# The last expert's gate and up weights ahead of expert 30's down weights, and the overflow branch ahead of the last column blocks

## The chip, the core and the metric

The kernel runs on one core of a Trainium2 chip. The metric is the device time of one launch in microseconds (us). A core has engines with instruction streams of their own: PE (TensorE, matrix products; PEld is its weight load, PEq and PEldq its sequencer), DVE (VectorE), ACT (ScalarE), POOL (GpSimd) and SP (SyncE, which here issues the DMAs). An engine executes its stream in order; engines wait for each other on semaphores.

## The reference

One decoder layer on 256 tokens of width 2048: RMSNorm, one input projection, differential attention beside a pooling mixer, one output projection and a residual, a second RMSNorm, a mixture of 32 gated experts, and a final RMSNorm. The part that matters here:

```python
coarse = xt @ w_coarse + b_coarse;  gsel = argmax(coarse)        # one of 4 groups
fine_sel = (xt @ w_fine[g] + b_fine)[tok, gsel]                  # 8 experts of the group
top_v, top_i = lax.top_k(fine_sel, 2)                            # 2 experts per token
for g in range(4):
    hg = einsum('td,edf->tef', xt, w_gate[sl]);  hu = einsum('td,edf->tef', xt, w_up[sl])
    h = silu(hg) * hu * combine[:, sl, None]
    y = y + einsum('tef,efd->td', h, w_down[sl])
return rmsnorm(h + y, final_norm_g)
```

An expert has 4 MB of gate, 4 MB of up and 4 MB of down weights; the 32 experts have 384 MB.

## The kernel before

All weights are streamed in units of 1 MB, 12 for an expert: 8 for gate and up (row tiles j = 0 to 3 of each) and 4 for down. SP issues them in the order of the code into a ring of 17 buffers. DMAs go over 8 semaphore lanes in turn, so the issue of one waits until the one 8 before it has landed.

Each expert has 32 token slots. `gather` brings the tokens of 4 experts together. For an expert `e`:

- `expert_in`: 32 products (tile `gu`) as the gate and up units land; the sums of each go through a copy (`part`) and 4 transposing products (`hT`), then silu and a multiplication give `hs`.
- `way_back`: the small tiles `bk` and `ws` that carry slots back to tokens (tile `pb`).
- `expert_out` (line 687, all experts but the last): 16 products `pd` over the four down units, `weighted` (line 683 on ACT gives `eoh`, line 684 on DVE `eol`), then 16 products `py` (line 699), and 8 additions to `y` on DVE (line 701). `py` uses the 4 PSUM banks of `psB`, so from the fifth on a `py` waits for an addition.

The last expert, 31, is written apart. `GU_ORDER[1]` loads and uses its four gate units before its four up units. Its down weights are cut by columns, not by rows of the sum: three units of 512 columns and two halves of 256. For each block, `down` (line 718) makes `pd31n` and its weighting, and `add_up` (line 727) makes the products and line 728 the additions; `square_sum` (lines 711, 708) sums the squares. `load_root` (line 188) loads the scalar engine's table for the square root ahead, and `keep_warm` puts 40 products that nothing reads on PE. `final_rstd` makes the norm's factor. Then comes the overflow branch: each engine loads the fullest expert's count (line 857) and jumps over `overflow` (line 859) when no expert has more than 32 tokens, which is the case with these inputs. The scaled rows go out at lines 866 and 868.

A scheduler at build time may move instructions within a stretch of code, but not over the branch. On the path that is not taken each engine raises its semaphores by what `overflow` would have added (the EVENT_SEMAPHORE rows of line 859), after its own earlier work is done; what other engines wait for beyond the branch counts from there.

Of the kernel before, what the change touches and what calls it, by code (L numbers as in the profile page):

```python
# [9 lines left out]
F32 = mybir.dt.float32  # L10
# [7 lines left out]
P = 128  # L18
T = 2            # token tiles
S = 256          # tokens  # L20
D = 2048
KT = D // P      # 16
NCK = 512        # columns of a weight chunk
# [3 lines left out]
NG = 4           # expert groups  # L27
EG = 8           # experts of a group
NE = NG * EG
FF = 512  # L30
NR = NG + NE     # router columns
C = 32           # token slots of an expert
EB = P // C      # experts whose slots are gathered at once
EPS = 1e-6
GU_ORDER = ([(j, m) for j in range(4) for m in range(2)], [(j, m) for m in range(2) for j in range(4)])
WINDOWS = (2, 4, 8, 16)
LAM_INIT = 0.8 - 0.6 * math.exp(-0.3 * 0)
N1, N2, N3 = 8, 7, 2     # units of the weight stream: throughout, after in_proj, after out_proj
AHEAD = 3                # steps by which the weights are split before their products
# [3 lines left out]
def hybrid_block(ctx: ExitStack, tc: tile.TileContext, x, xT, par, lam4d, rbias, w_in, pool_w, w_out, w_out_b,  # L43
# [32 lines left out]
    def load_unit(src, name):  # L76
        """Some row tiles of a chunk of weights."""
        u = wunit(name).rearrange("p (k n) -> p k n", k=src.shape[1])
        nc.sync.dma_start(u, src)
        return u  # L80

    # the chunks of columns, in the order of the work: v, q, k, q, k, u, u, and w_out
    views = [w_in[c] for c in (4, 5, 0, 2, 1, 3, 6, 7)] + [w_out[c] for c in range(3)] + [w_out_b[c] for c in range(2)]
    # the order of the row tiles: w_out's wait for the heads and pools
# [37 lines left out]
    def keep_warm(rhs, n, name):  # L122
        """Products that nothing reads: the tensor engine's clock drops when it idles."""
        pw_ = bank(name)
        for _ in range(n):
            nc.tensor.matmul(pw_[:, 0:rhs.shape[-1]], ones_b, rhs, start=True, stop=True)
# [6 lines left out]
    # -dist for (q0,k0) | (q1,k0) (q1,k1)  # L133
# [7 lines left out]
    # tri[s, t] = 1 where s <= t  # L141
# [4 lines left out]
    iota_s = const.tile([P, EB, C], F32, name="iota_s")      # 1 + place, EB times  # L146
    nc.gpsimd.iota(iota_s, pattern=[[0, EB], [1, C]], base=1, channel_multiplier=0,
                   allow_small_or_imprecise_dtypes=True)
    # low[i, j] = 1 where j < i
# [4 lines left out]
    iota_m = const.tile([P, NG], F32, name="iota_m")       # i - 4  # L154
    nc.gpsimd.iota(iota_m, pattern=[[1, NG]], base=-NG, channel_multiplier=0,
                   allow_small_or_imprecise_dtypes=True)
    # sel[32 j + s, s'] = (s == s')
# [5 lines left out]
    def rsqrt(pool, dst, ssq, n, tag):  # L163
        """dst = (ssq / n + eps) ** -0.5, elementwise, by Newton's steps from a bit-level seed."""
        shp = list(ssq.shape)
        a = pool.tile(shp, F32, tag=tag + "a", name=tag + "a")
        nc.vector.tensor_scalar(a, ssq, 1.0 / n, EPS, op0=OP.mult, op1=OP.add)
        h = pool.tile(shp, I32, tag=tag + "h", name=tag + "h")
        nc.vector.tensor_scalar(h, a.bitcast(I32), 1, None, op0=OP.logical_shift_right)
        nc.vector.tensor_scalar(dst.bitcast(I32), h, -1.0, float(0x5F3759DF), op0=OP.mult, op1=OP.add)  # L170
        q = pool.tile(shp, F32, tag=tag + "q", name=tag + "q")
        for _ in range(3):
            nc.vector.tensor_mul(q, dst, dst)
            nc.vector.scalar_tensor_tensor(q, q, -0.5, a, op0=OP.mult, op1=OP.mult)
            nc.vector.scalar_tensor_tensor(dst, q, 1.5, dst, op0=OP.add, op1=OP.mult)

    def rsqrt_of(dst, a, tag):
        """dst = a ** -0.5: the scalar engine's root, the reciprocal, a Newton step."""
        q = const.tile(list(a.shape), F32, tag=tag + "q", name=tag + "q", bufs=2)
        nc.scalar.activation(q, a, AF.Sqrt)  # L180
        nc.vector.reciprocal(dst, q)
        nc.vector.tensor_mul(q, dst, dst)
        nc.vector.scalar_tensor_tensor(q, q, -0.5, a, op0=OP.mult, op1=OP.mult)
        nc.vector.scalar_tensor_tensor(dst, q, 1.5, dst, op0=OP.add, op1=OP.mult)

    def load_root(after):
        """The scalar engine's table for the root, ahead of its use."""
        nc.scalar.activation(const.tile([P, 1], F32, tag="root", name="root", bufs=2), after, AF.Sqrt, scale=0.0)

# [18 lines left out]
    def split(s_):  # L208
        """Weights in two parts that a single pass each carries exactly."""
# [12 lines left out]
    def multiply(s_):  # L222
# [6 lines left out]
        for kk in range(ks):  # L229
# [4 lines left out]
            if c < 2 or c >= 8:            # tokens x columns: the activations stand  # L234
# [5 lines left out]
            else:                          # columns x tokens: the weights stand  # L240
# [7 lines left out]
    # what goes along with each step  # L248
# [8 lines left out]
    # 1 / rms of the tokens, as a column and along the rows  # L257
# [41 lines left out]
    def _():  # L299
        # lambda  # L300
# [7 lines left out]
        # router weights times the norm's gain  # L308
        nc.vector.tensor_tensor(wr, wr, g2c[:, :, None].to_broadcast([P, KT, NR]), op=OP.mult)
        # 1 / (t + 1) of the first tokens  # L310
# [7 lines left out]
    def evac_qk(c, i):  # L318
        """Half i (0 queries, 1 keys) of the heads 4 c to 4 c + 3."""
# [9 lines left out]
    def scores(h):  # L329
# [14 lines left out]
        nm = front.tile([P, 2, 2], F32, tag="nm", name=f"nm{h}", bufs=2)       # [t, c]  # L344
# [202 lines left out]
    # the group: the first of the largest  # L547
# [13 lines left out]
    # an expert's rank: how many are larger, or as large and earlier  # L561
# [18 lines left out]
    slot = small("slot", T, NE)         # 1 + place among the expert's tokens, or 0  # L580
    nc.vector.tensor_tensor(slot, pos[:, 0:2 * NE].rearrange("p (t e) -> p t e", t=T), mskf, op=OP.mult)

# [4 lines left out]
    # where the stream's units go: what is free early first; the y tiles follow the units in mpool  # L587
# [12 lines left out]
    def load_expert(e):  # L600
        gu, ds = ([], []), []
        for j, m in GU_ORDER[e == NE - 1]:
            for v in ((gate_v, up_v)[m],):
                gu[m].append(unit(f"w{'gu'[m]}{e}_{j}").rearrange("p (k f) -> p k f", k=4))
                nc.sync.dma_start(gu[m][-1], v[e, :, 4 * j:4 * j + 4, :])
        for j in range(4):
# [3 lines left out]
            else:  # L610
                ds[-1] = ds[-1].rearrange("p (f n) -> p f n", f=4)
                for c0 in range(0, NCK, NCK if j < 3 else NCK // 2):
                    cs = slice(c0, c0 + (NCK if j < 3 else NCK // 2))
                    nc.sync.dma_start(ds[-1][:, :, cs],
                                      down_v[e, :, :, j * NCK + cs.start:j * NCK + cs.stop].rearrange("f p n -> p f n"))
        return gu, ds

    def gather(b):
        """The slots of EB experts: their tokens' rows, transposed; in four steps."""
# [18 lines left out]
    def expert_in(e, xe, gu, step=None):  # L638
        """silu(x gate) * (x up), transposed."""
        i = e % EB  # L640
        acc = [psA.tile([P, 512], F32, tag="acc", name=f"gu{e}{m}") for m in range(2)]
        for j, m in GU_ORDER[e == NE - 1]:
# [17 lines left out]
    def way_back(e):  # L660
        """[slot, token] EB times, and the slots' weights."""
# [14 lines left out]
    def weighted(pd, ws_, n, name, last=False):  # L676
        """The slots' outputs times their weights, in two parts that a single pass each carries exactly."""
# [35 lines left out]
    def down(e, hs, ds, ws_, n):  # L713
        """Some columns of the last expert's way out, in four parts of the sum over f."""
# [7 lines left out]
    def add_up(e, bk, eo, n, t):  # L722
        """The way back adds the parts up."""
# [12 lines left out]
    def overflow(hnT):  # L736
        """Tokens beyond an expert's slots: every expert over all tokens, weighted by what the slots left out."""
# [9 lines left out]
        for t in range(T):  # L747
# [34 lines left out]
            for n in range(5):  # L782
                square_sum(t, n)
        final_rstd()

    ws = {0: load_expert(0)}
    xe, step, routed = gather(0)
    keep_warm(hot, 18, "warm2")
    ws[1] = load_expert(1)
    y = [mpool.tile([P, D], F32, tag="m", name=f"y{t}", bufs=4) for t in range(T)]  # L790
    hs0 = expert_in(0, xe, ws[0][0], step)

    def weigh():
        """Weights of the chosen experts, and the fullest expert's count."""
# [29 lines left out]
    for e in range(NE):  # L824
        if 1 < e + 1 < NE:
            ws[e + 1] = ws.get(e + 1) or load_expert(e + 1)
# [4 lines left out]
        gu, ds = ws.pop(e)  # L831
        hs = expert_in(e, xe, gu) if e else hs0
        bk, ws_ = way_back(e) if e else bk0
        if e < NE - 1:
            expert_out(e, hs, ds, bk, ws_)
        if e == NE - 4:
            # the last norm's gain, on all partitions
            gf = mpool.tile([P, D], F32, tag="m", name="gf", bufs=4)
            for n in range(4):
# [5 lines left out]
                nc.scalar.copy(gf[:, n * NCK:(n + 1) * NCK], pgf)  # L845
    load_root(hs[:, 0, 0:1])
    ss3 = const.tile([P, T], F32, name="ss3")
    rstd3 = const.tile([P, T], F32, name="rstd3")
    keep_warm(ones_b, 40, "warm3")
# [7 lines left out]
    n_most = nc.values_load(most_i[0:1, 0:1], min_val=0, max_val=S)  # L857
    hnT = mpool.tile([P, KT, P], F32, tag="m", name="hnT", bufs=4)
    with tc.If(n_most > C):
        overflow(hnT)  # L860

# [13 lines left out]
def _layout(i):  # L875
    """The inputs as the kernel reads them: rows and columns moved, nothing computed."""
    import numpy as np
    a = {k: np.asarray(v) for k, v in i.items()}
    rows = lambda v: v.reshape(P, KT)                  # d = p * 16 + k
    tiles = lambda v: v.reshape(-1, P).T               # d = k * 128 + p  # L880
# [41 lines left out]
```

## Time and profile before

| | us |
|---|---|
| three timed runs, median | 1266.39 (1266.08 to 1267.1) |
| span of the profiled execution | 1267.7 |
| last SP weight issue (last half unit of expert 31's down weights) | 1235.5 |
| first `pd31` product | 1242.57 |
| last sum of squares on ACT ends | 1255.27 |
| first scaled row on DVE | 1257.71 |

The page gives no total for the profiled execution beside its span, which is 1.3 us above the median of the timed runs. PE is busy 87% of the span and the 16 DMA engines carry 365 GB/s on average, but the average hides three stages: the projections (PE and DVE), the experts (the weight stream), and the tail after the last weights. Times of rows below count from the start of the span.

### The profile page before, as it was taken

To read this page: it belongs to the slowest core of one execution; us is meant where nothing else is said; L and a number is where in the kernel's file an instruction comes from. 1 tells how busy PE (TensorE), PEld (TensorE's weight loads), DVE (VectorE), ACT (ScalarE), POOL (GpSimd) and SP (SyncE) were. 2 spreads that over 40 slices of the span, in tenths; PEclk is the share of its full clock that TensorE was granted. 3 is DMA by queue.
4 is the path that set the end of the run, shared out by engine and by line. 5 is a ranking of instruction groups with operands and counts; after the bars stand their busy time and mean duration, and the time that the engine had idled before them with its cause. 6 is when DMAs were issued, how large, how long until landed. Compare 5 with 4: busy or idle time off the path is not lost. (4 is left out here: it accounts for less than half of the span.)

```text
span 1267.7 us, 17150 instructions
## 1 busy us (share of the span) xinstructions
PE 1102.7 (87%) x7043; PEld 651.6 (51%) x7043; DVE 498.9 (39%) x1046; ACT 232.7 (18%) x503; POOL 2.1 (0%) x13
## 2 busy tenths in 40 slices
PE   9999999999998988887788779877977888888875
PEld 6899999889733622442263326323632352244222
DVE  6657788654342223232232222222332313222325
ACT  6545555444000000000000000000000000000103
POOL 0000000000000000000000000000000000000000
PEclk9999999999998979898779877977997787879977
DMA  9954443795899999999999999999999999999994
GB/s 375 357 179 167 159 142 134 298 370 207 335 420 421 420 421 421 421 421 421 421 420 421 421 422 422 420 421 421 421 421 421 421 420 421 421 421 421 421 412 146
DMA packets 67957, 464.10 MB, mean 366 GB/s; under 512 B 7584, under 2 KB 8992, under 8 KB 12576
## 3 DMA queue, kind: packets, MB, share of 16 engines
q1 hardware_dynamic: 67728, 462.92, 89.9%
q8 instruction: 57, 0.93, 0.3%
q14 instruction: 28, 0.23, 0.0%
q10 hardware_dynamic: 144, 0.01, 0.0%
HBM read 460.81 MB, written 2.10 MB: 365 GB/s over the span
## 5 line engine op out<-in xcount | busy, mean ns | idle before, releaser
L647 PE MATMUL gu<-wg,xe 128*32 128x512 f32 x1024 | 211.7, 651 | 14.8 <-DMA wg<-in_w_gate_dram 14.8
L647 PE MATMUL gu<-wu,xe 128*32 128x512 f32 x1024 | 196.7, 650 | 9.9 <-DMA wu<-in_w_up_dram 9.9
L691 PE MATMUL pd<-wd,hs 128*32 128x512 f32 x992 | 157.5, 787 | 25.9 <-DVE hs L657 19.3
L219 DVE TENSOR_TENSOR wlo<-w,whi 128x512 fp32r<-128x512 f32 x192 | 131.1, 689 | 82.3 <-ACT whi L218 81.5
L701 DVE TENSOR_TENSOR y<-y,py 128x512 f32<-128x512 f32 x240 | 148.2, 681 | 31.1 <-PE py L699 30.2
L218 ACT CAST whi<-w 128x512 fp32r<-128x512 f32 x192 | 117.9, 619 | 116.7 <-PE acc L246 56.7
L654 PEld LDWEIGHTS hT<-sel,part 128*128 128x128 f32 x512 | 74.6, 224 | 112.8 <-DVE part L652 56.5
L654 PE MATMUL hT<-sel,part 128*128 128x32 f32 x512 | 82.1, 309 | 45.6 <-DVE part L652 23.6
L632 PEld LDWEIGHTS pg<-ohr,h 128*128 128x128 f32 x512 | 112.7, 311 | 6.4 <-DVE y L701 3.9
L632 PE MATMUL pg<-ohr,h 128*128 128x128 f32 x512 | 114.7, 393 | 0.0
L671 DVE CAST bk<-pb 128x256 fp32r<-128x256 f32 x32 | 13.6, 425 | 256.7 <-PE pb L669 256.7
L699 PE MATMUL py<-eoh,bk 32*128 32x512 f32 x248 | 78.0, 550 | 41.1 <-ACT eoh L683 25.0
L652 ACT COPY part<-gu 128x512 f32<-128x512 f32 x32 | 18.8, 586 | 500.3 <-PE gu L647 500.3
L246 PE MATMUL acc<-xhi,whi 128*128 128x256 f32 x384 | 110.1, 287 | 0.0
L246 PE MATMUL acc<-xhi,wlo 128*128 128x256 f32 x384 | 108.7, 283 | 0.0
L246 PE MATMUL acc<-xlo,whi 128*128 128x256 f32 x384 | 108.4, 282 | 0.0
L684 DVE SCALAR_TENSOR_TENSOR eol<-pd,ws,eoh 128x512 fp32r<-128x512 f32 x31 | 23.3, 750 | 192.8 <-ACT eoh L683 192.8
L691 PEld LDWEIGHTS pd<-wd,hs 128*32 128x32 f32 x992 | 35.9, 138 | 122.8 <-issue 79.6
L647 PEld LDWEIGHTS gu<-wg,xe 128*32 128x32 f32 x1024 | 42.1, 114 | 102.9 <-issue 64.6
L699 PEld LDWEIGHTS py<-eoh,bk 32*128 32x128 f32 x248 | 30.7, 199 | 114.7 <-DVE y L701 59.4
L647 PEld LDWEIGHTS gu<-wu,xe 128*32 128x32 f32 x1024 | 40.0, 115 | 77.8 <-issue 54.1
L246 PEld LDWEIGHTS acc<-xhi,whi 128*128 128x128 f32 x384 | 72.6, 189 | 2.4 <-ACT aT L366 2.0
(213 smaller groups left out, 1114.7 us busy)
## 6 DMA issues: line engine op xcount, KB each, us to landing
wg<-in_w_gate_dram SPq DMA_DIRECT2D x128, 1024.0 KB, 19.8
wu<-in_w_up_dram SPq DMA_DIRECT2D x128, 1024.0 KB, 19.8
wd<-in_w_down_dram SPq DMA_DIRECT2D x127, 1024.0 KB, 19.8
w<-in_w_in_dram SPq DMA_DIRECT2D x31, 1024.0 KB, 5.7
w<-in_w_out_dram SPq DMA_DIRECT2D x12, 1024.0 KB, 4.9
w<-in_w_out_b_dram SPq DMA_DIRECT2D x4, 1024.0 KB, 6.0
x<-in_x_dram SPq DMA_DIRECT2D x2, 1024.0 KB, 18.4
h<-in_x_dram SPq DMA_DIRECT2D x2, 1024.0 KB, 8.5
```

The lines of the kernel that those rows point to most:

```text
L218: nc.scalar.copy(hi, w)
L219: nc.vector.tensor_sub(lo, w, hi.bitcast(F32))
L246: nc.tensor.matmul(o, l, r, start=b, stop=e, skip_group_check=True)
L632: nc.tensor.matmul(pg_[:, kk * P:(kk + 1) * P], ht[t][:, 4 * k4 + kk::KT], ohr[:, t].rearrange("p e s -> p (e s)"), start=(t == 0), stop=( ...
L647: nc.tensor.matmul(acc[m][C * kk:C * (kk + 1), :], xe[:, 4 * j + kk, i * C:(i + 1) * C], gu[m][j][:, kk, :], start=(j == 0), stop=(j == 3))
L652: (nc.scalar.copy if m == 0 else nc.vector.tensor_copy)(part, acc[m])
L654: nc.tensor.matmul(hT[:, m, f, :], part[:, f * P:(f + 1) * P], sel, start=True, stop=True)
L671: nc.vector.tensor_copy(bk, pb[:, 0:S].rearrange("p (t s) -> p t s", t=T))
L684: nc.vector.scalar_tensor_tensor(lo, pd[:, 0:n], ws_, hi.bitcast(F32), op0=OP.mult, op1=OP.subtract)
L691: nc.tensor.matmul(pd[C * n:C * (n + 1), :], hs[:, f, :], ds[f][:, n * NCK:(n + 1) * NCK], start=(f == 0), stop=(f == 3))
L699: nc.tensor.matmul(ps, bk[rows, t, :], eo[i][rows, :], start=(i == 0), stop=(i == 1))
L701: nc.vector.tensor_add(y[t][:, cs], (ht if e == 0 else y)[t][:, cs], ps)
```

## The change

The loads of an expert are cut into `load_in` (gate, up) and `load_out` (down). For expert 31, `load_in` stands right behind `load_in(30)`, ahead of `load_out(30)`; its gate and up units alternate like every other expert's. In the loop, `expert_in(31)` and `way_back(31)` stand ahead of `expert_out(30)`. The branch stands behind `expert_out(30)` and ahead of the last expert's column blocks. The 40 products of `keep_warm` are gone. The sums of squares and `final_rstd` inside `overflow` are gone, since the ordinary ones now follow it. Comments are removed.

```diff
-GU_ORDER = ([(j, m) for j in range(4) for m in range(2)], [(j, m) for m in range(2) for j in range(4)])
+GU_ORDER = [(j, m) for j in range(4) for m in range(2)]
...
-            for n in range(5):
-                square_sum(t, n)
-        final_rstd()
...
-    for e in range(NE):
-        if 1 < e + 1 < NE:
-            ws[e + 1] = ws.get(e + 1) or load_expert(e + 1)
+    for e in range(NE - 1):
+        if 1 < e + 1 < NE - 1:
+            ins[e + 1] = load_in(e + 1)
+            if e + 1 == NE - 2:
+                ins[NE - 1] = load_in(NE - 1)
+            outs[e + 1] = load_out(e + 1)
+        if e == NE - 2:
+            outs[NE - 1] = load_out(NE - 1)
...
-        if e < NE - 1:
-            expert_out(e, hs, ds, bk, ws_)
+        if e == NE - 2:
+            hs_z = expert_in(NE - 1, xe, ins.pop(NE - 1))
+            bk_z, ws_z = way_back(NE - 1)
+        expert_out(e, hs, outs.pop(e), bk, ws_)
...
+    n_most = nc.values_load(most_i[0:1, 0:1], min_val=0, max_val=S)
+    hnT = mpool.tile([P, KT, P], F32, tag="m", name="hnT", bufs=4)
+    with tc.If(n_most > C):
+        overflow(hnT)
+    e, hs, bk, ws_, ds = NE - 1, hs_z, bk_z, ws_z, outs.pop(NE - 1)
     load_root(hs[:, 0, 0:1])
-    keep_warm(ones_b, 40, "warm3")
     eo = down(e, hs, ds, ws_, 0)
     for n in range(5):
         nxt = down(e, hs, ds, ws_, n + 1) if n < 4 else None
         for t in range(T):
             add_up(e, bk, eo, n, t)
         eo = nxt
     final_rstd()
-    n_most = nc.values_load(most_i[0:1, 0:1], min_val=0, max_val=S)
-    hnT = mpool.tile([P, KT, P], F32, tag="m", name="hnT", bufs=4)
-    with tc.If(n_most > C):
-        overflow(hnT)
```

PE before, behind expert 30's last up unit (`wu30_3`); `pd30` and `py30` are expert 30's way out:

```order
L647 MATMUL gu301_8338<-wu30_3_8187,xe7_7984 32x512 x4
L654 MATMUL hT30_8371<-sel_165,part1_30_8378 128x32 x4
L691 MATMUL pd30_8399<-wd30_0_8189,hs30_8384 32x512 x4
L691 MATMUL pd30_8399<-wd30_1_8191,hs30_8384 32x512 x4
L691 MATMUL pd30_8399<-wd30_2_8193,hs30_8384 32x512 x4
L691 MATMUL pd30_8399<-wd30_3_8195,hs30_8384 32x512 x4
L699 MATMUL py30_00_8420<-eoh30_8416,bk30_8395 128x512
```

PE at the same place now:

```order
L651 MATMUL gu301_8338<-wu30_3_8187,xe7_7984 32x512 x4
L658 MATMUL hT30_8371<-sel_165,part1_30_8378 128x32 x4
L651 MATMUL gu310_8399<-wg31_0_8189,xe7_7984 32x512 x4
...
L651 MATMUL gu311_8400<-wu31_3_8203,xe7_7984 32x512 x4
L658 MATMUL hT31_8433<-sel_165,part1_31_8440 128x32 x4
L695 MATMUL pd30_8461<-wd30_0_8205,hs30_8384 32x512 x4
L695 MATMUL pd30_8461<-wd30_1_8207,hs30_8384 32x512 x4
L695 MATMUL pd30_8461<-wd30_2_8209,hs30_8384 32x512 x4
L695 MATMUL pd30_8461<-wd30_3_8211,hs30_8384 32x512 x4
```

All of expert 31's gate and up work has moved ahead of expert 30's way out. PE before, at the first column block (`pd310`, `pd311`):

```order
L647 MATMUL gu311_8453<-wu31_3_8326,xe7_7984 32x512 x4
L654 MATMUL hT31_8486<-sel_165,part1_31_8493 128x32 x4
L718 MATMUL pd310_8559<-wd31_0_8328,hs31_8499 32x512 x4
L718 MATMUL pd311_8567<-wd31_1_8330,hs31_8499 32x512 x4
L727 MATMUL py31_00_8575<-eo31_0_8564,bk31_8510 128x512 x2
```

PE now, from expert 30's last products over the branch to the same block (what is left out is `overflow`):

```order
L703 MATMUL py30_13_8510<-eoh30_8478,bk30_8395 128x512
L703 MATMUL py30_13_8510<-eol30_8479,bk30_8395 128x512
L854 TENSOR_LOAD most_i_3857
L856 COMPARE_AND_BRANCH
...
L856 UNCONDITIONAL_BRANCH
L722 MATMUL pd310_9134<-wd31_0_8328,hs31_8446 32x512 x4
L722 MATMUL pd311_9142<-wd31_1_8330,hs31_8446 32x512 x4
L731 MATMUL py31_00_9150<-eo31_0_9139,bk31_8457 128x512 x2
```

What stands right ahead of the first block was the gate and up work of the same expert; now it is the way out of expert 30 and the jump. ACT before, at the last sum of squares and the root of the final norm:

```order
L711 ACTIVATE sq331_8645,ssq3_3872<-y1_3744 128x256
L711 ACTIVATE sq340_8651,ssq3_3872<-y0_3743 128x256
L180 ACTIVATE n3q_8661<-ss3_8516 128x2
L857 TENSOR_LOAD most_i_3857
L859 COMPARE_AND_BRANCH
```

ACT now, behind the branch and at the same place:

```order
L856 UNCONDITIONAL_BRANCH
L687 ACT_TABLE_LOAD
L687 ACTIVATE eo31_0_9139<-pd310_9134,ws31_8459 128x512
...
L715 ACTIVATE sq340_9226,ssq3_3872<-y0_3743 128x256
L180 ACT_TABLE_LOAD
L180 ACTIVATE n3q_9236<-ss3_9132 128x2
L925 UNCONDITIONAL_BRANCH
```

`load_root`'s table load stays ahead of the branch; two more table loads stand behind it, one before the first block and one before the root.

## Rows read from the trace of the kernel before

**Rows 1.** The page: bandwidth in 40 equal slices of the span.

```profile
GB/s 375 357 179 167 159 142 134 298 370 207 335 420 421 420 421 421 421 421 421 421 420 421 421 422 422 420 421 421 421 421 421 421 420 421 421 421 421 421 412 146
```

**Rows 2.** Stretches: length, busy time by engine, granted clock, DMA share, GB/s.

```profile
core 0: us, PE busy (x) PEld busy (x) DVE busy (x) ACT busy (x) POOL busy (x), PEclk, DMA share, GB/s
1190.00:1200.00 10.00, 8.32 (x62) 2.59 (x61) 5.00 (x8) 0.69 (x1) 0.00 (x0) 1.00 1.02 422
1215.00:1220.00 5.00, 2.39 (x11) 0.49 (x11) 0.47 (x1) 0.69 (x1) 0.00 (x0) 0.61 1.01 416
1220.00:1225.00 5.00, 4.65 (x15) 1.28 (x12) 3.36 (x6) 0.00 (x0) 0.00 (x0) 0.50 1.01 419
1246.00:1247.00 1.00, 1.00 (x4) 0.65 (x2) 0.34 (x1) 0.20 (x1) 0.00 (x0) 0.60 0.04 15
```

**Rows 3.** Timeline, SP: the issue of expert 31's last up unit; line 605: its landing.

```profile
1216.78 0.33 SPq L605 DMA_DIRECT2D wu<-in_w_up_dram  x1
...
DMA to landing us min/median/max: 19.7/19.7/19.7
```

**Rows 4.** Timeline, expert 31's last up products to its first column block and norm.

```profile
1237.20 2.78 PE L647 MATMUL gu<-wu,xe 128*32 128x512 f32 x24
1242.21 1.28 ACT L188 ACT_TABLE_LOAD   x1
1242.57 2.90 PE L718 MATMUL pd<-wd,hs 128*32 128x512 f32 x16 [0.69 <-DVE hs L657]
1243.51 0.20 ACT L188 ACTIVATE root<-hs 128x1 f32<-128x1 f32 x1
1252.24 1.80 PE L727 MATMUL py<-eo,bk 128*128 128x256 f32 x8
1255.08 0.19 ACT L711 ACTIVATION_READ_ACCUMULATOR sq<-y 128x1 f32 x1
1255.84 0.20 ACT L180 ACTIVATE n3q<-ss 128x2 f32<-128x2 f32 x1 [0.57 <-DVE ss L733]
1257.71 5.39 DVE L866 SCALAR_TENSOR_TENSOR y<-y,rstd,gf 128x256 f32<-128x256 f32 x8 [0.89 <-DVEq L859]
```

**Rows 5.** Timeline, the way out of expert 30.

```profile
1216.76 1.94 PE L691 MATMUL pd<-wd,hs 128*32 128x512 f32 x8 [2.26 <-DMA wd<-in_w_down_dram]
1218.81 0.69 ACT L683 ACTIVATE eoh<-pd,ws 128x512 fp32r<-128x512 f32 x1 [8.11 <-PE pd L691]
1221.16 3.08 DVE L701 TENSOR_TENSOR y<-y,py 128x512 f32<-128x512 f32 x5 [0.88 <-PE py L699]
1223.05 1.92 PE L647 MATMUL gu<-wg,xe 128*32 128x512 f32 x2
1226.16 1.88 DVE L701 TENSOR_TENSOR y<-y,py 128x512 f32<-128x512 f32 x3 [1.92 <-PE py L699]
```

**Rows 6.** Timeline, the way out of expert 29.

```profile
1189.86 3.64 PE L691 MATMUL pd<-wd,hs 128*32 128x512 f32 x32 [0.69 <-DVE hs L657]
1195.68 5.03 DVE L701 TENSOR_TENSOR y<-y,py 128x512 f32<-128x512 f32 x8 [0.59 <-PE py L699]
1198.39 0.55 PE L699 MATMUL py<-eol,bk 32*128 32x512 f32 x3
```

**Rows 7.** Lines 857 and 859, the branch: engine, instruction, duration in ns, start.

```profile
L857 PEldq TENSOR_LOAD <-most_i x1: 487/487/487, 1253.4 to 1253.4; - x1
...
L859 SPq COMPARE_BRANCH  x1: 50/50/50, 1237.4 to 1237.4; - x1
L859 PEldq COMPARE_BRANCH  x1: 3862/3862/3862, 1254.0 to 1254.0; - x1
L859 ACTq COMPARE_BRANCH  x1: 45/45/45, 1256.4 to 1256.4; - x1
L859 DVEq COMPARE_BRANCH  x1: 72/72/72, 1257.3 to 1257.3; - x1
L859 PEldq EVENT_SEMAPHORE  x1: 51/51/51, 1257.9 to 1257.9; - x1
```

More of the change, by code (lines that the diff above doesn't have):

```diff
@@ L598, in unit, with load_in, load_out @@
         return pool.tile([P, 2048], F32, tag=r, name=name, bufs=bufs)
[L600 to L605, printed above, removed]
+    def load_in(e):
+        gu = ([], [])
+        for j, m in GU_ORDER:
+            gu[m].append(unit(f"w{'gu'[m]}{e}_{j}").rearrange("p (k f) -> p k f", k=4))
+            nc.sync.dma_start(gu[m][-1], (gate_v, up_v)[m][e, :, 4 * j:4 * j + 4, :])
+        return gu
+    def load_out(e):
+        ds = []
         for j in range(4):
@@ L609, in load_expert @@
                 nc.sync.dma_start(ds[-1], down_v[e, j])
[L610 to L616, printed above, removed]
+                continue
+            ds[-1] = ds[-1].rearrange("p (f n) -> p f n", f=4)
+            w = NCK if j < 3 else NCK // 2
+            for c0 in range(0, NCK, w):
+                nc.sync.dma_start(ds[-1][:, :, c0:c0 + w],
+                                  down_v[e, :, :, j * NCK + c0:j * NCK + c0 + w].rearrange("f p n -> p f n"))
+        return ds
     def gather(b):
@@ L641, in expert_in @@
         acc = [psA.tile([P, 512], F32, tag="acc", name=f"gu{e}{m}") for m in range(2)]
-        for j, m in GU_ORDER[e == NE - 1]:
+        for j, m in GU_ORDER:
             if step and m == 0:
@@ L781, in overflow @@
                     nc.vector.scalar_tensor_tensor(y[t][:, cs], po, ccol, y[t][:, cs], op0=OP.mult, op1=OP.add)
-            for n in range(5):
-                square_sum(t, n)
-        final_rstd()
-    ws = {0: load_expert(0)}
+    ins, outs = {0: load_in(0)}, {0: load_out(0)}
     xe, step, routed = gather(0)
     keep_warm(hot, 18, "warm2")
-    ws[1] = load_expert(1)
+    ins[1], outs[1] = load_in(1), load_out(1)
     y = [mpool.tile([P, D], F32, tag="m", name=f"y{t}", bufs=4) for t in range(T)]
-    hs0 = expert_in(0, xe, ws[0][0], step)
+    hs0 = expert_in(0, xe, ins.pop(0), step)
     def weigh():
@@ L830, in hybrid_block @@
                 step(j)
-        gu, ds = ws.pop(e)
-        hs = expert_in(e, xe, gu) if e else hs0
+        hs = expert_in(e, xe, ins.pop(e)) if e else hs0
         bk, ws_ = way_back(e) if e else bk0
-        if e < NE - 1:
-            expert_out(e, hs, ds, bk, ws_)
+        if e == NE - 2:
+            hs_z = expert_in(NE - 1, xe, ins.pop(NE - 1))
+            bk_z, ws_z = way_back(NE - 1)
+        expert_out(e, hs, outs.pop(e), bk, ws_)
         if e == NE - 4:
```

## The prediction, made before the changed kernel was run

> **What bounds the kernel now.** I read the page's 40 slices first. From the twelfth slice on the bandwidth stands at 420 to 422 GB/s until the last two slices [rows 1]: the experts are bound by the weight stream. A unit of 1.049 MB takes 1.049 / 421 = 2.49 us there. The change moves no byte in or out, so what it can win or lose lies behind the point where the stream ends. The stretches by engine come next: between 1246 and 1247 us the stream is at 15 GB/s, so it is over [rows 2], and the span ends at 1267.7. These 21 us are the tail, and only they can move.
>
> In the tail I read the timeline backwards from the first scaled row at 1257.71 [rows 4]. It follows the branch on DVE (0.89 us of idle time), the norm's root on ACT at 1255.84, the last sum of squares, which ends at 1255.08 + 0.19 = 1255.27, and the column blocks, which begin at 1242.57. Before that first product stands the chain of expert 31: its up products end at 1237.20 + 2.78 = 1239.98, then copy, transposes, silu. The last up unit had landed at 1216.78 + 19.7 = 1236.48 [rows 3]. So from the last gate or up unit to the first column block there are 1242.57 - 1236.48 = 6.1 us, then 12.7 us of blocks, then the norm, the branch and the output.
>
> **The change part by part.** *Order of the stream.* Expert 31's eight units come ahead of expert 30's four. All 12 have the same size and the same contiguous lines, and the buffers that they and the last down units reuse were last read by expert 30's gate and up products or earlier work. I cost the swap itself at nothing: expert 30's last down unit takes the place of expert 31's last up unit and lands at 1236.48; expert 31's down units keep their places and the stream its end. Expert 31's last up unit now lands four units earlier, about 1226.5, and its `hs` is ready some 4 us later (about 1 us of products, then the 2.6 us that lay between 1239.98 and 1242.57), well ahead of need.
>
> *The 6.1 us chain goes.* Behind the landing at 1236.48 there is no gate or up work left.
>
> *What is late next.* PE works in order, and expert 30's way out now stands there. Its price has two rows. In the way out of expert 30 before, the last down unit's products began at 1216.76 and the first addition at 1221.16, 4.40 us later; five additions took 3.08 us, 0.62 each [rows 5]. That was at a granted clock of 0.50 to 0.61, its lower level (1.2 GHz) for most of the stretch, behind a PE that had waited for weights: 2.39 us busy in the 5 us from 1215 [rows 2]. In the way out of expert 29, at a granted clock of 1.00, the last quarter of the `pd` products began at about 1189.86 + 0.75 x 3.64 = 1192.6 and the additions at 1195.68, 3.1 us later; all eight took 5.03 us, and PE was through at 1198.39 + 0.55 = 1198.94, 1.77 us before the last of them [rows 2, 6]. After the change PE waits for one unit every 2.49 us from about 1236.5 - 11 x 2.49 = 1209 on, with four products for each, as it did before the stretch at the lower level; without the 40 filler products (they filled time in which PE waited, and cost nothing) it is idle even more. So I take the lower level: first addition at 1236.48 + 4.40 = 1240.9, last one done at 1240.9 + 8 x 0.62 = 1245.8, PE through at 1245.8 - 1.77 = 1244.0. In rows 5 the last three additions came late because PE had products of expert 31 in between (1223.05); these are gone. At the upper level it would be 1239.6, 1244.6 and 1242.8.
>
> *The branch on PE.* This is a wait that the change puts on the path. Before, PE reached the branch when it had nothing more to do: its last product ended at 1252.24 + 1.80 = 1254.04, the jump lasted 3862 ns, and PE was behind it at 1257.95, 3.9 us after its last product [rows 7]. ACT, DVE and SP jumped in 45 to 72 ns. PE is the one with several hundred instructions to jump over. Now all column blocks are queued behind this jump, and ACT and DVE wait for them. I carry the 3.9 us over: first block at 1244.0 + 3.9 = 1247.9. The bounds: 0.1 us if PE jumps like the others; then DVE decides, which must finish its additions and its own branch (0.89 us) first, at 1245.8 + 0.9 = 1246.7. On the other side, a second stop of the same length, if the code behind the jump does not come in one piece or comes slower beside the stream: 1251.8. I take the one row that shows PE at this jump.
>
> The Trainium skill ("Advanced Engine Details and Errata", Control Flow Timing) has a compare-and-branch at about 108 ns. The trace is below that on three engines and 36 times above it on PE; by the page the first block would begin where DVE lets it, and the sum below would be 1.2 us smaller.
>
> *The other engines at the branch.* ACT is through early, since its last work ahead of it is the weighting of expert 30. SP has only the output behind it. DVE's 0.9 us end by 1246.7, under PE's jump. Cost: nothing, while PE's jump lasts; without it DVE's is the one that shows, as said.
>
> *The blocks.* The same instructions as before, by data that has landed before 1247 [rows 2], 12.7 us. Two things can differ. The first 16 products took 2.90 us; at the lower level they take twice 1.94 = 3.9 [rows 5], at the upper one half of 3.64 = 1.8 [rows 6]. PE comes out of 4 us without a product, so I expect the lower level at the start and add 0.5 us, with -1.1 and +2 as the bounds (the last one if the lower level lasts through more blocks; the end of the blocks is paced by the sums of squares on ACT, which don't hang on it).
>
> *The end.* The branch is gone from DVE's path between the norm's factor and the first scaled row: -0.89 + 0.03 = -0.86. But ACT now loads a table between its last sum of squares and the root: `load_root`'s load is followed by a second one behind the branch, which stands early and is hidden, and a third at the root. Last sum 1255.27 + 1.28 = 1256.55, where the root ran at 1255.84 before: +0.71. Together -0.15.
>
> The Trainium skill ("ScalarE: Activation LUTs", What ACT_TABLE_LOAD costs) gives a switch 2.66 us, the load of 1.28 and a drain of 1.38. The trace has the 1.28, and the next activation at 1243.51 begins 0.02 us behind it [rows 4], so no drain shows here; with it the sum would be 1.4 us larger.
>
> **The sum.** First block 1247.9 instead of 1242.57: +5.3. Blocks +0.5, end -0.15: +5.7. The profiled span would be 1273.4 instead of 1267.7. The median of the timed runs, 1266.39, is 1.3 us below that span, and the page shows no other total; the same 5.7 us on the median give **1272.1 us**, slower by 0.45%.
>
> **The rivals.**
>
> *The jump is cheap on PE.* For it: the three other engines in the rows jump in under 0.1 us [rows 7], and the row of 3862 ns is from an engine with nothing left to do. Against: PE alone skips so much code. First block 1246.7, +4.1 + 0.5 - 0.15: 1270.8.
>
> *PE keeps the upper clock.* For it: the way out of expert 29 ran at 1.00. Against: PE was busy 8.32 of the 10 us around it, and only 2.39 of 5 in the paced stretch at 1215, which is the nearer likeness [rows 2]. PE through at 1242.8, first block 1246.7, +4.1, blocks -0.8: 1269.5.
>
> *PE stops twice for code* or longer, beside the end of the stream. +3.9 on the forecast: 1276.0. The trace of before has one such stop only, at a time without traffic.
>
> *Not slower: the chain that goes is what counts.* One mechanism: `hs` of expert 31 is there by 1231, so the blocks run as their units land, and expert 30's way out with the jump fits into the 6.1 us that the old chain took. Place: PE between 1236.5 and the first block. If the first block stays at 1242.6, the blocks run at the upper level (-0.8) and the end wins 0.15: 1265.4. It decides if PE is past the jump by about 1243.5; up to 1245.9 the result stays within 0.2%. Against it: the best row of a way out, at the full clock, needs 6.3 us on PE from the last landing (3.1 + 5.03 - 1.77), and its jump comes on top.
>
> **How the numbers follow.** Forecast 0.50, cheap jump 0.13, upper clock 0.14, two stops 0.15, not slower 0.08. Within 0.2% (2.5 us, about what a measurement of this kernel can tell from no change) means 1263.9 to 1268.9. "Not slower" gives 0.03 to faster and 0.05 to the same, and 0.03 of the upper clock falls below 1268.9. So faster 0.03, same 0.08, slower 0.89. The range from 1268.6 to 1276.6 leaves out most of the last rival below and a part of the two stops above.
>
> **What would show it.** In the new trace: the last down unit of expert 30 lands near 1236.5, and its way out on DVE ends near 1246; PE's COMPARE_BRANCH lasts near 3.9 us and ends near 1248; the first block follows it at once; a table load of 1.28 us stands between ACT's last sum of squares and the root; the first scaled row follows the factor without a branch. The stream's rate and end don't move. I am wrong if PE's jump is short, if the way out ends by 1243, or if the stream ends more than 1 us elsewhere.

## The result and the profile after

The changed kernel took 1274.28 us (median; 1272.71 to 1275.71), the kernel before beside it 1266.24 (1265.8 to 1267.1). The ratio is 1.0064 [1.0049, 1.0078]: slower by 8.0 us, with 6.2 to 9.9 as the interval. The forecast was 1272.1, the range 1268.6 to 1276.6. In the experiments below, one slow execution of e7 (1944 us) is left out of its ratio.

The traced execution has a span of 1273.5 us and was timed at 1275.71, so 2.2 us lie outside the span. Three of its stretches, to be held against [rows 2]:

```profile
1215.00:1220.00 5.00, 4.36 (x36) 0.87 (x28) 0.00 (x0) 0.00 (x0) 0.00 (x0) 0.84 1.02 419
...
1231.00:1236.00 5.00, 4.49 (x24) 2.45 (x28) 0.75 (x2) 1.76 (x3) 0.00 (x0) 0.50 0.98 365
...
1244.00:1248.00 4.00, 0.36 (x1) 0.00 (x0) 1.81 (x4) 0.00 (x0) 0.00 (x0) 0.50 0.13 40
```

From 1231 to 1236, where expert 30's 32 `pd` products begin, the granted clock is 0.50, the lower level; from 1237 to 1243, the rest of that way out, it is 1.00. Between 1244 and 1248 PE works 0.36 us: a hole that the kernel before had only behind its last product. The timeline of the same stretch, which answers to [rows 4, 5]; the first row is SP's, the issue of expert 31's five down units:

```profile
1218.29 17.38 SPq L618 DMA_DIRECT2D wd<-in_w_down_dram  x5
...
1228.77 1.93 PE L651 MATMUL gu<-wu,xe 128*32 128x512 f32 x8
...
1231.52 1.91 PE L658 MATMUL hT<-sel,part 128*128 128x32 f32 x8 [0.81 <-DVE part L656]
...
1233.36 5.45 PE L695 MATMUL pd<-wd,hs 128*32 128x512 f32 x32
...
1238.89 0.69 ACT L687 ACTIVATE eoh<-pd,ws 128x512 fp32r<-128x512 f32 x1 [3.63 <-PE pd L695]
...
1239.98 1.28 ACT L687 ACT_TABLE_LOAD   x1 [0.41 <-DMA wd<-in_w_down_dram]
...
1240.94 4.87 DVE L705 TENSOR_TENSOR y<-y,py 128x512 f32<-128x512 f32 x8 [0.59 <-PE py L703]
...
1243.81 0.55 PE L703 MATMUL py<-eol,bk 32*128 32x512 f32 x1
...
1248.18 3.64 PE L722 MATMUL pd<-wd,hs 128*32 128x512 f32 x16 [3.81 <-PEq L856]
...
1261.37 0.19 ACT L715 ACTIVATION_READ_ACCUMULATOR sq<-y 128x1 f32 x1
1261.58 1.28 ACT L180 ACT_TABLE_LOAD   x1
1262.87 0.20 ACT L180 ACTIVATE n3q<-ss 128x2 f32<-128x2 f32 x1
...
1263.89 5.39 DVE L874 SCALAR_TENSOR_TENSOR y<-y,rstd,gf 128x256 f32<-128x256 f32 x8
```

Read it at the brackets: the first column block at 1248.18 waited 3.81 us for PE's own sequencer at line 856, the branch. The branch itself, by line (engine, duration in ns, start), which answers to [rows 7]:

```profile
L856 ACTq COMPARE_BRANCH  x1: 45/45/45, 1239.4 to 1239.4; - x1
...
L856 PEldq COMPARE_BRANCH  x1: 3794/3794/3794, 1244.1 to 1244.1; - x1
L856 DVEq COMPARE_BRANCH  x1: 72/72/72, 1245.0 to 1245.0; - x1
```

The Trainium skill ("Runtime: NRT & Kernel Launch", Instruction fetch mechanics) says that a taken branch to code that is not yet in the engine's instruction memory stalls until it is fetched, and gives no price. The trace agrees; the price on PE here is 3.35 to 3.86 us in nine of the eleven traces that jump over all of `overflow`, and 6.23 and 6.28 us in the other two (e6, e2).

### The profile page after: what moved, and what is told of

It is laid out like the page before. It is cut to its first block, busy times and chain, and to the rows that moved or that the text cites. A ratio compares the mean times of both kernels' runs of the same rounds, so it can differ in the third digit from the quotient of the medians.

```text
span 1273.5 us, 17081 instructions
## 1 busy us (share of the span) xinstructions
PE 1108.1 (87%) x7003; PEld 650.6 (51%) x7003; DVE 498.5 (39%) x1046; ACT 235.2 (18%) x505; POOL 2.1 (0%) x13
## 5 line engine op out<-in xcount | busy, mean ns | idle before, releaser
L651 PE MATMUL gu<-wg,xe 128*32 128x512 f32 x1024 | 223.3, 665 | 13.4 <-DMA wg<-in_w_gate_dram 13.4
L651 PE MATMUL gu<-wu,xe 128*32 128x512 f32 x1024 | 206.4, 659 | 8.8 <-DMA wu<-in_w_up_dram 8.8
L705 DVE TENSOR_TENSOR y<-y,py 128x512 f32<-128x512 f32 x240 | 148.1, 681 | 37.8 <-PE py L703 37.4
L658 PE MATMUL hT<-sel,part 128*128 128x32 f32 x512 | 80.6, 306 | 45.6 <-DVE part L656 23.6
L703 PE MATMUL py<-eoh,bk 32*128 32x512 f32 x248 | 81.2, 575 | 41.4 <-ACT eoh L687 24.1
```

Of the source, the lines that this page charges most:

```text
L651: nc.tensor.matmul(acc[m][C * kk:C * (kk + 1), :], xe[:, 4 * j + kk, i * C:(i + 1) * C], gu[m][j][:, kk, :], start=(j == 0), stop=(j == 3))
L658: nc.tensor.matmul(hT[:, m, f, :], part[:, f * P:(f + 1) * P], sel, start=True, stop=True)
L703: nc.tensor.matmul(ps, bk[rows, t, :], eo[i][rows, :], start=(i == 0), stop=(i == 1))
L705: nc.vector.tensor_add(y[t][:, cs], (ht if e == 0 else y)[t][:, cs], ps)
```

## The experiments

Executions start their stream up to 2 us apart, so traces are compared from one event: the issue of expert 31's first down unit (the SP row above). The table gives, in us behind that issue, the first column block, the first scaled row and the end of the span; each is one subtraction in a trace.

| kernel | issue | block | scaled | end | ratio to before, timed |
|---|---|---|---|---|---|
| before, trace of the prediction | 1219.09 | 23.5 | 38.6 | 48.6 | |
| before, second (e8) | 1217.71 | 21.1 | 36.3 | 46.2 | 1.0006 [0.9994, 1.0017] |
| before, third (e9) | 1218.37 | 21.1 | 37.0 | 47.1 | 0.9999 [0.9988, 1.0010] |
| changed | 1218.29 | 29.9 | 45.6 | 55.2 | 1.0064 [1.0049, 1.0078] |
| changed, second (e10) | 1218.10 | 29.7 | 44.2 | 53.9 | 1.0059 [1.0036, 1.0082] |
| order alone (e1) | 1216.94 | 24.6 | 40.8 | 50.8 | 1.0022 [1.0003, 1.0040] |
| branch alone (e2) | 1218.95 | 30.7 | 44.8 | 54.5 | 1.0057 [1.0036, 1.0079] |
| branch alone, no filler (e6) | 1217.59 | 27.2 | 42.1 | 51.8 | 1.0035 [1.0022, 1.0048] |
| changed, root behind branch (e3) | 1218.86 | 30.3 | 43.9 | 53.5 | 1.0048 [1.0033, 1.0063] |
| changed, short jump (e4) | 1218.81 | 28.0 | 43.4 | 52.6 | 1.0030 [1.0013, 1.0047] |
| before, no filler (e5) | 1217.99 | 21.9 | 37.4 | 47.2 | 1.0004 [0.9995, 1.0013] |
| changed, filler back (e7) | 1216.98 | 28.5 | 44.3 | 53.9 | 1.0048 [1.0035, 1.0062] |

**e1: the new order, the branch at the end as before.**

```diff
+            for n in range(5):              # back inside overflow
+                square_sum(t, n)
+        final_rstd()
...
-    n_most = nc.values_load(...)        # ahead of the column blocks
...
-    with tc.If(n_most > C):
-        overflow(hnT)
...
     final_rstd()
+    n_most = nc.values_load(...)
...
+    with tc.If(n_most > C):
+        overflow(hnT)
```

> The changed kernel with the branch put back to the end (the sums of squares inside the overflow put back too): only the order of loads and work is new, and the filler products are gone. Theory (way out of expert 30 and PE's jump each carry a part): the first column block starts when PE is through with expert 30's products, near 1244.4 us by the trace, 1.8 us later than before; no table load at the root, and the branch is back on DVE in front of the first scaled row (0.9 us). Time +2 to +3 us against the kernel before, ratio 1.0015 to 1.0025. Rival A (the order alone is what costs, PE's jump is hidden beside it): +5 us or more, ratio above 1.004. Rival B (the order is a gain, only the jump costs): below 0.999.

Measured 1270.21 us, by the ratio +2.8 [0.4, 5.1]: as the theory had it, though the interval just reaches Rival A's +5. Its timeline:

```profile
1234.38 1.07 PE L695 MATMUL pd<-wd,hs 128*32 128x512 f32 x8 [1.44 <-DMA wd<-in_w_down_dram]
...
1237.87 4.87 DVE L705 TENSOR_TENSOR y<-y,py 128x512 f32<-128x512 f32 x8 [0.88 <-PE py L703]
...
1241.55 3.64 PE L722 MATMUL pd<-wd,hs 128*32 128x512 f32 x16
```

Here expert 30's last products wait for the landing and take 1.07 us; PE goes from the way out straight into the block. Without the jump the new order costs 3.5 us at the first block (24.6 against 21.1). One thing besides the branch differs from the changed kernel's trace: the granted clock while PE does expert 31's gate and up work. The same stretch here, then in the changed kernel:

```profile
1224.00:1234.00 10.00, 6.59 (x54) 2.91 (x53) 1.47 (x4) 1.76 (x3) 0.00 (x0) 1.00 1.02 401
```

```profile
1224.00:1234.00 10.00, 8.45 (x42) 5.13 (x38) 1.41 (x4) 1.10 (x3) 0.00 (x0) 0.50 1.01 402
```

It is 0.50 to 0.51 in all five traces with the new order and the new place of the branch (changed, e10, e3, e4, e7). PE is through with expert 30's products 24.7 us behind the issue here, and 26.1 and 26.2 us in the two traces of the changed kernel.

**e2: the old order, the branch ahead of the blocks.**

```diff
-            for n in range(5):              # inside overflow
-                square_sum(t, n)
-        final_rstd()
...
+    n_most = nc.values_load(...)
...
+    with tc.If(n_most > C):
+        overflow(hnT)
     load_root(hs[:, 0, 0:1])
...
     keep_warm(ones_b, 40, "warm3")
...
     final_rstd()
-    n_most = nc.values_load(...)
...
-    with tc.If(n_most > C):
-        overflow(hnT)
```

> The kernel before with nothing changed but the branch, which stands ahead of the last expert's column blocks. Theory: PE jumps for 3.8 us right behind the last up products' transposes (about 1241.9), so the first block starts near 1245.8 instead of 1242.6, +3.2; the blocks start at the lower clock, +0.5; a table load in front of the root and no branch there, -0.15. Time +3 to +4.5 us, ratio 1.0024 to 1.0036. Rival A (the order carries all): within 0.5 us, ratio about 1.000. Rival B (the branch carries all): +5.5 us or more, ratio above 1.0043.

Measured 1274.25, +7.2 [4.6, 10.0]: more than expected, and the price that Rival B named. The timeline shows the two reasons that the expectation missed:

```profile
1236.38 1.07 PE L647 MATMUL gu<-wu,xe 128*32 128x512 f32 x8 [1.48 <-DMA wu<-in_w_up_dram]
...
1245.31 4.42 PE L126 MATMUL warm<-ones_b 128*128 128x128 bf16 x40 [5.98 <-PEq L845]
1249.67 2.70 PE L718 MATMUL pd<-wd,hs 128*32 128x512 f32 x16
```

The jump took 6.28 us, and the 40 products that nothing reads now stood behind it: 4.4 us at the lower clock, on the path.

**e6: e2 without those 40 products.**

```diff
-    keep_warm(ones_b, 40, "warm3")
```

> Order of the kernel before, the branch ahead of the column blocks, and the 40 products that nothing reads left out. With them this kernel had a jump of 6277 ns (1238.9 to 1245.2), the filler behind it for 4.4 us and the first block at 1249.67. Theory (the jump and the filler add up on PE): first block near 1245.2 to 1245.5, limited by the end of the jump, 4.2 us earlier; end of the run 3 to 4 us earlier than with the filler, ratio to the kernel before 1.002 to 1.0035. Rival (the filler only fills a wait for something else, for example DVE's and SP's own way past the branch): first block near 1248 or later, ratio 1.0045 to 1.006.

Measured 1271.39, +4.4 [2.8, 6.1]; the upper end of the theory's range. PE's branch in e6, by line:

```profile
L845 PEldq COMPARE_BRANCH  x1: 6234/6234/6234, 1238.2 to 1238.2; - x1
```

The first block came right behind it, at 1244.75, behind the issue 0.6 to 0.9 us later than expected. So the branch alone costs 6.1 us at the block (27.2 against 21.1), the jump being the long one.

**e4: most of the products in `overflow` left out, so that the jump is short.** This leaves out part of the computation on the path that these inputs don't take.

```diff
-        for t in range(T):
+        for t in range(1):
-            for k4 in range(4):
+            for k4 in (0, 3):
-                    for k in range(KT):
+                    for k in (0, KT - 1):
-                    for f in range(4):
+                    for f in (0, 3):
```

> The changed kernel with most of the overflow's products left out (one token tile, 2 of 16 row tiles, half of the way out), so that the code that PE jumps over is about a tenth; the branch isn't taken with these inputs. Theory (the 3.8 us are the fetch of code far away): PE's COMPARE_BRANCH falls below 0.2 us, the first block then waits for DVE's additions and branch and starts near 1246.3 instead of 1248.2; time about -2 us against the changed kernel, ratio near 1.003 to 1.0045. Rival (PE's jump costs the same whatever its length, since PE first has to drain): COMPARE_BRANCH near 3.8 us, no change.

Measured 1271.38, 2.9 us below the changed kernel's median in the first comparison and 2.1 below that in the last; the ratio, 1.0030, lies within what the theory gave. By line:

```profile
L856 PEldq COMPARE_BRANCH  x1: 368/368/368, 1245.0 to 1245.0; - x1
...
L856 DVEq COMPARE_BRANCH  x1: 72/72/72, 1245.8 to 1245.8; - x1
L856 DVEq EVENT_SEMAPHORE  x1: 21/21/21, 1246.8 to 1246.8; - x1
```

and the first block in its timeline:

```profile
1246.84 3.64 PE L722 MATMUL pd<-wd,hs 128*32 128x512 f32 x16 [1.72 <-DVEq L856]
```

The branch instruction is the same and PE's work ahead of it too; only the code skipped is shorter (32 products instead of 320), and 3794 ns became 368, not quite the 200 that the theory had as its upper end. Now PE stands 1.72 us for DVE's own way past the branch, so only half of the 3.4 us comes back (first block at 28.0 against 29.9). In the 5 us from 1244 the instruction queue q8 moved two packets in the changed kernel and one here (DMA view of both, the row of that queue):

```profile
q8 instruction: 2, 0.03, 2.9%
```

```profile
q8 instruction: 1, 0.02, 1.2%
```

Cut into windows of 0.1 us, the changed kernel's first packet moves at 1245.0, inside PE's jump (1244.1 to 1247.9); the one here moves at 1246.1, after the jump is over.

**e3: `load_root` reads a value that exists only behind the branch, so that its table load can't move ahead.**

```diff
-    load_root(hs[:, 0, 0:1])
+    load_root(y[0][:, 0:1])
```

> The changed kernel with the early use of the square root made to read y, which the branch may write, so that it can't be moved ahead of the branch: one table load behind the branch serves the blocks and the root. Theory: the load in front of the root (1.28 us) goes, and the root runs 0.7 us earlier: the stretch from the last sum of squares to the first scaled row falls from 2.3 to about 1.6 us; time -0.7 us against the changed kernel, ratio about 1.0040 to 1.0058 against the kernel before. Rival (the table load is hidden beside the last reduction anyway): no change of that stretch, same time as the changed kernel.

Measured 1272.99, ratio 1.0048, within the theory's range. In its timeline the root waits for the norm's sum and no table load precedes it:

```profile
1260.99 0.19 ACT L715 ACTIVATION_READ_ACCUMULATOR sq<-y 128x1 f32 x1
1261.75 0.20 ACT L180 ACTIVATE n3q<-ss 128x2 f32<-128x2 f32 x1 [0.57 <-DVE ss L737]
```

From the last sum (1261.18) to the root it is 0.57 us here and 1.31 in the changed kernel: the 0.7 us are shown in the trace. In the times the two intervals overlap, so there the step is not told from nothing.

**e5: the kernel before without the 40 filler products** (the edit of e6).

> The kernel before without the 40 products that nothing reads (keep_warm). In its trace they take 1.05 + 1.51 = 2.56 us of PE between 1233.78 and 1237.27, and expert 31's up products end at 1239.98, 3.50 us behind the last up unit's landing (1236.48); in the run with the branch alone, where the products that nothing reads stand elsewhere, the up products end at 1237.45. Theory (the filler delays the tail, the prediction's 'cost nothing' is wrong): up products end near 1237.5 and the first block begins near 1240.1; what the tail wins is at most these 2.5 us, less where the last down units' landings pace the blocks: 1 to 2.5 us faster, ratio 0.998 to 0.9992. Rival (the filler keeps the upper clock, so it is worth its time): granted clock at the lower level in the up products or the first blocks, ratio 1.000 to 1.002.

Measured 1267.24 against 1266.32: +0.5 [-0.6, 1.6]. The theory fails. The rival's ratio and its sign are there, with a granted clock of 0.50 in the first block (1237 to 1243), but the interval holds no change, and e8 below, with the filler, has most of its first block at the lower level too (0.50 from 1239 to 1241): no run shows the filler to be worth anything. But the block stood at 21.9 here and at 23.5 in the trace that the prediction was made from, with the same median time. That puts the trace of before in doubt.

**e8 and e9: the kernel before, unchanged, traced twice more.**

> The kernel before, a second trace. Its first trace is of an execution some 3 us above the median (span 1267.7, mean granted clock 0.876; timed executions with spans near 1264 show clocks of 0.89). From the issue of expert 31's first down unit to the end it took 1267.7 - 1219.1 = 48.6 us; the kernel without filler took 47.2 by the same measure and yet has the same median. Theory (the first trace caught a long tail): an execution near the median has a tail of about 47 us, so that the changed kernel's 55.2 is about 8 us more, as timed. Rival (the tail is always 48.6, and the median executions are shorter ahead of it): tail 48.3 to 48.9, issue near 1216.

> The kernel before, a third trace, for the spread of its tail. Theory: between 46.5 and 49 us from the issue of expert 31's first down unit to the end, shorter where the granted clock of the last column blocks and of expert 31's last products is the upper level. Rival: 48.6 within 0.3.

Both have the first block 21.1 us behind the issue, 2.4 us earlier than the first trace, and tails of 46.2 and 47.1: the theory of e8 holds and both rivals fail. e8 was timed at 1265.87 with a span of 1263.9, which is 1.97 outside; the execution of the prediction, with 1267.7, was then one of some 1269.7 us, 3 above the median. Its mean granted clock is 0.887, not the 0.876 of the expectation, and e8's is 0.887 too: what differs is where the lower level falls. The timeline of e8:

```profile
1229.43 1.05 PE L126 MATMUL warm<-ones_b 128*128 128x128 bf16 x16
...
1231.41 1.51 PE L126 MATMUL warm<-ones_b 128*128 128x128 bf16 x24
...
1232.86 1.93 PE L647 MATMUL gu<-wu,xe 128*32 128x512 f32 x16
...
1235.17 1.07 PE L647 MATMUL gu<-wu,xe 128*32 128x512 f32 x8 [0.39 <-DMA wu<-in_w_up_dram]
...
1238.81 3.39 PE L718 MATMUL pd<-wd,hs 128*32 128x512 f32 x16 [0.69 <-DVE hs L657]
...
1253.97 5.39 DVE L866 SCALAR_TENSOR_TENSOR y<-y,rstd,gf 128x256 f32<-128x256 f32 x8 [0.89 <-DVEq L859]
```

The last eight up products wait 0.39 us for their unit, which lands at 1235.1: PE is on time, done 1.1 us behind the landing, and the block begins 3.7 us behind it. In [rows 4] the last 24 products ended 3.50 us behind the landing (1239.98 - 1236.48): PE was late there. That they stand in one row without a wait does not show it; e9 has such a row as well,

```profile
1234.00 2.89 PE L647 MATMUL gu<-wu,xe 128*32 128x512 f32 x24
```

and ends 1.1 us behind its landing (1235.8), with the block again 3.7 us behind. The stretches of two traces show where PE fell behind; first the kernel before as predicted from, then e8:

```profile
1222.00:1225.00 3.00, 3.00 (x7) 0.69 (x7) 2.24 (x4) 0.00 (x0) 0.00 (x0) 0.50 1.01 421
1225.00:1228.00 3.00, 3.00 (x18) 1.01 (x22) 1.84 (x3) 0.00 (x0) 0.00 (x0) 0.50 1.01 420
1228.00:1231.00 3.00, 3.00 (x22) 0.63 (x14) 0.04 (x1) 0.00 (x0) 0.00 (x0) 0.71 1.01 402
```

```profile
1222.00:1225.00 3.00, 3.00 (x19) 0.71 (x19) 1.88 (x3) 0.00 (x0) 0.00 (x0) 0.55 1.02 423
1225.00:1228.00 3.00, 2.24 (x19) 0.56 (x12) 0.00 (x0) 0.58 (x1) 0.00 (x0) 1.00 1.02 412
1228.00:1231.00 3.00, 3.00 (x38) 2.46 (x38) 0.49 (x2) 0.00 (x0) 0.00 (x0) 1.00 1.01 400
```

Both executions fall to the lower level (1.2 GHz) in this stretch; in e8 the clock is back at 1225, 7 us behind the issue, in the first trace only after 1229, 10 us behind it, and PE, busy without a gap up to 1231, carried the delay on to the first block. In e9 it is at the upper level from 1217 to 1240.

**e10: the changed kernel, traced again.**

> The changed kernel, a second trace; the first is of its slowest timed execution. Theory (PE's jump and the way out of expert 30 are on the path in each execution): jump 3.5 to 4 us, first block at once behind it, tail from the issue of expert 31's first down unit 53.5 to 55.5 us, the lower value where PE runs expert 30's products at the upper clock. Rival (the lower clock of the first trace is a chance of that execution, and the loss usually smaller): upper clock at expert 30's way out, tail 52 to 53 us.

```profile
1218.08 1.06 PE L651 MATMUL gu<-wg,xe 128*32 128x512 f32 x8 [1.41 <-DMA wg<-in_w_gate_dram]
1220.57 1.93 PE L651 MATMUL gu<-wu,xe 128*32 128x512 f32 x8 [1.43 <-DMA wu<-in_w_up_dram]
...
1233.30 5.61 PE L695 MATMUL pd<-wd,hs 128*32 128x512 f32 x32
...
1247.84 3.45 PE L722 MATMUL pd<-wd,hs 128*32 128x512 f32 x16 [3.50 <-PEq L856]
```

The same picture: eight products grow from 1.06 to 1.93 us at 1220, behind a PE that waited 1.4 us for each unit, and the 32 products of the way out begin at the lower level (0.50 from 1231 to 1236); from 1237 on it is the upper level here too (0.97 to 1243). The jump took 3354 ns, a little under the expected 3.5 us. Tail 53.9, inside what the theory gave.

**e7: the filler put back into the changed kernel, ahead of expert 31's gate and up work.**

```diff
+            keep_warm(ones_b, 40, "warm3")
             hs_z = expert_in(NE - 1, xe, ins.pop(NE - 1))
```

> The changed kernel with the 40 products put back, ahead of expert 31's gate and up work. Theory (the missing filler has no share in the loss): PE's jump and the first block stay within 1 us (1247.5 to 1249), ratio to the kernel before 1.005 to 1.0075. Rival (PE fell to the lower clock because the filler is gone, and the way out of expert 30 is late for that): with the filler the granted clock is 1.00 at the way out, PE is through near 1242.8 and the first block begins near 1246.7, ratio 1.003 to 1.005. If the filler delays PE further, the first block comes up to 2.5 us later and the ratio is 1.0075 to 1.009.

Inconclusive. The time (1.0048) is the rival's, though its interval reaches into the theory's range; the trace is not: the block, 28.5 us behind the issue, is at the theory's lower end, and PE's products of expert 30 still took 5.28 us, not the 3.64 of the upper level. They only began 1.0 to 1.2 us sooner behind the issue (14.0 against 15.1 and 15.2):

```profile
1219.45 1.07 PE L651 MATMUL gu<-wu,xe 128*32 128x512 f32 x8 [1.43 <-DMA wu<-in_w_up_dram]
1221.93 1.06 PE L651 MATMUL gu<-wg,xe 128*32 128x512 f32 x8 [1.42 <-DMA wg<-in_w_gate_dram]
...
1231.02 5.28 PE L695 MATMUL pd<-wd,hs 128*32 128x512 f32 x32
```

Whether that microsecond is the filler's or chance, one trace can't say. No run beats the kernel before; e5 equals it with less code.

## Why the prediction was right, and where its sum was off

The sign, the place and the mechanism held: the loss is expert 30's way out and then PE's jump, both ahead of the first block. Its size, +5.7 against +8.0 measured, was off mainly by one term, the chain below (2.4 us too much taken away). Two smaller misses cancel, which is luck: against the issue PE came to the first block 1.0 us later than the sum had it, and behind the first block the changed kernel lost 1.1 us less (-0.8 against +0.35).

- *The swap of the stream at nothing.* Held. Expert 30's last down unit was issued at 1215.8 and landed 19.9 us later, 17.4 us behind the common issue; 17.4 was predicted (1236.48 - 1219.09).
- *"Behind the landing at 1236.48 there is no gate or up work left": the 6.1 us chain.* This term was mis-sized. The chain that goes is 3.7 us in e8 and in e9, from the landing to the first block. The other 2.4 us were the delay of one execution. The prediction named the filler products as something that filled waits of PE; in that trace PE had no waits there, and its last products ended 3.50 us behind the landing, where 1.1 us is usual. The span's 1.3 us over the median was taken as the whole difference, though the time outside the span was not shown; by the later runs it is 2 us more.
- *The way out at the lower clock.* The level was right for the `pd` products up to 1237 (0.50) and wrong behind that (1.00), and the additions ran from 1240.94 to 1245.81 against 1240.9 to 1245.8. Partly by luck: the stream was 0.8 us earlier in this execution. The last products weren't paced by the landing, as assumed, but stood in a queue from 1233.36 on, behind expert 31's late transposes. Behind the issue that is 0.8 us later than the sum had it. The argument from PE's waits to the lower level is not borne out as it stands: e1, with the same order and also without the filler, did expert 31's work at 1.00.
- *The jump.* 3.9 carried over, 3.79 and 3.35 measured. e4 refutes the rival in which PE waits there for something else; it also shows that the bound for a cheap jump, DVE's way past the branch, was right within 0.4 us (27.6 behind the issue worked out, 28.0 found).
- *Blocks and end.* From first block to last sum 13.4 and 12.2 us in the two traces, 13.2 predicted; but the kernel before itself has 12.7 and 13.5 in e8 and e9, so the added 0.5 does not show, although the first 16 products did run mostly at the lower level (3.64 and 3.45 us). From last sum to first scaled row 2.33 against 2.44 before: -0.11 for -0.15, the table load against the branch as worked out. The next activation begins 0.01 us behind the load; the drain that the Trainium skill ("ScalarE: Activation LUTs", What ACT_TABLE_LOAD costs) adds does not show.
- *The rivals.* No second stop for code behind the jump and no cheap jump. The upper clock came at 1237, behind most of the `pd` products of the way out. "Not slower" needed PE past the jump by 1243.5; it was 1247.9.

Against e8 and e9, the two later traces of before, the account closes: first block +8.7 (29.8 against 21.1), first block to first scaled row -0.4 (means of 15.1 and 15.5), the rest -0.4 (9.6 against 10.0), together +7.9; timed +8.0 and +7.5. The 8.7 us at the block are 3.5 for the order at e1's clock, 1.5 by which PE is later through with expert 30 than in e1 (26.2 against 24.7), and 3.7 for the jump. The 1.5 us go with the lower level; e1 is one trace, so what they depend on is not shown. e6's 6.1 us are not a part of this sum, since its jump was the long one.

Open: why the jump took 6.2 us in e2 and e6. Both began at 1238 to 1239 with the stream still running, but e7's began at 1241.6, also ahead of the stream's end, and took 3.6. The traces show where the time lies. In the nine shorter jumps the first packet on q8 moves 0.9 to 1.4 us after the jump begins, in e2 and e6 3.6 us after it; from the packet to the end of the jump it is 2.4 to 2.9 us in all eleven. e2's is at 1242.5 (DMA view, 1242.5 to 1242.6):

```profile
q8 instruction: 1, 0.02, 69.2%
```

In the microsecond in which the jumps of e2 and e6 began, the DMA engines still moved 376 and 293 GB/s, and 192 in e7's. That the fetch queued behind the weights would fit; no run tests it.

## What to carry to other kernels

A taken branch over much code cost the engine that skips it 3.4 to 6.3 us here, not the 45 to 72 ns of the other engines; leave it where that engine has nothing behind it, or make the skipped code short. A chain removed ahead of a stage is worth only what the next queue on the same engine doesn't need. Before a sum is made against one trace, see how long after the landing of its data the work ends that the sum takes away: 3.50 us in the first trace, 1.1 us in two others of the same kernel. A delay that a second trace doesn't have is not the kernel's usual cost.

## What was not expected of the hardware

PE's jump took 368 ns over a tenth of the products of `overflow`, 3354 to 3862 over all of them, and 6234 and 6277 in the two kernels of the old order with the branch ahead of the blocks; with two lengths of code measured, whether it grows with the length or steps up is open. Between executions of the same kernel, the stretch at the lower clock ended 3 us apart or more, and the first block moved by 2.4 us with it.
